# Routed experts in 32-token units with block transposes on VectorE and 21 weight buffers

## The chip, the core and the metric

The kernel runs on one core of a Trainium2 chip. A core has a matrix engine (PE, or TensorE, with a queue for weight loads that the profile lists as PEld), VectorE (DVE), ScalarE (ACT), GpSimd (POOL) and a queue engine SyncE (SP) that only issues DMA transfers here. SBUF holds data in 128 partitions, PSUM takes the matmul results. The metric is the device time of one execution in microseconds (us), the median over runs.

## The reference

One layer of an encoder over 1024 tokens with width 1024: a token mixer, a cross-attention, a mixture of 32 experts, a final norm. Only the experts matter here:

```python
g_logits = (h @ w_rg) + b_rg
p_top, g_idx = lax.top_k(softmax(g_logits), 1)          # 1 of 4 groups
e_top, e_local = lax.top_k(e_logits_of_that_group, 2)   # 2 of its 8 experts
weights = p_top * softmax(e_top)
...
y = (silu(xb @ w_gate[e]) * (xb @ w_up[e])) @ w_down[e]
out = zeros((T, D)).at[t_sorted].add(w_sorted[:, None] * y)
```

All is float32. An expert has w_gate and w_up of 1024 x 512 and w_down of 512 x 1024, 6 MB in all, and 32 of them have to be read from HBM in each execution: 201 MB. 2048 pairs of token and expert are spread over them by the routing, which only the data decide.

## The kernel before, in words

The mixer, the attention and the routing take the first 800 us or so. Behind them comes the expert stage, which is the one that changes.

**Blocks.** The stage walks through 33 blocks in the order of a string, ORDER. A letter says how many tokens of an expert a block can hold: A 96, N 64, B 128. T is an N that takes the first tokens of the busiest expert, and the B behind it the rest of them, with the same weights. The first four blocks (A) work on fixed experts. The later ones look their expert up in a table sorted by load (`perm`), by a register load on SP. Experts that would not fit run in a loop behind the blocks (`For_i`).

**Weights.** The weights of an expert come as 6 loads of 1 MiB, parts 0 to 3 with gate and up columns for two k-tiles of 128 rows each (L926), parts 4 and 5 with the rows of w_down (L928). They go into buffers named `wraw`; SEATS is their number, 20. SP issues the loads in the order of use. `free`, called behind each part, hands the buffer of a finished part to `prep_r`, which issues the next load.

**Tokens.** A gather on POOL (L1081) fetches up to 128 rows of the tokens' states, two blocks ahead. `xpose` turns them by 8 PE transposes (L1165) so that features lie on partitions. Two consecutive N blocks share one gather and one transpose.

**Matmuls.** The tokens are the stationary operand, the weights move. With 64 tokens stationary the array's 128 columns are used as two halves, each with 512 weight columns (`gh`, L1189, and `yh`, L1222). With 32 tokens it is four quarters of 256 weight columns (`gq`, `yq`, the same lines). An A block is a unit of 64 and one of 32 tokens, B two units of 64, N one of 64. `turn` has the units change places from part to part. A matmul of the program is float32 and shows as two records in the trace, each with its weight load.

**Between.** ACT takes silu of the gate columns (L1198), DVE multiplies by the up columns (L1199): `sg`. Then `mpose` brings `sg` into the shape of a stationary operand by PE transposes (L1207) into PSUM, and ACT and DVE copy the result into `mT` (L1210).

**Order on PE.** For block b: parts 0 and 1, the mpose of block b-1, parts 2 and 3, the `xpose` of block b+1, parts 4 and 5 of block b-1 (w_down). The instructions are put in place by a scheduler, but in the main in that order.

**Out.** `store` copies the results from PSUM into a row buffer (L1231; ACT for the unit of 64, DVE for the second unit), multiplies by the routing weight (L1233) and adds the rows to `acc` by an indirect DMA on POOL (L1234). After the last block SP reads `acc` back (L1467), and a last stage normalises and writes the output.

Of the kernel before, what the change touches and what calls it, by code (L numbers as in the profile page):

```python
# [44 lines left out]
ORDER = "AAAA" + "NNN" + "AN" * 4 + "TBN" + "BN" + "AN" * 2 + "AANAANANN"  # L45
NS = ORDER.count("N")
SEATS = 20
# [3 lines left out]
def tile_hybrid_encoder(ctx: ExitStack, tc: tile.TileContext,  # L51
# [1093 lines left out]
    with ExitStack() as pa:  # L1145
        rawp[2] = pa.enter_context(tpool(name="raw5", bufs=SEATS - 11))
        mc = pa.enter_context(tpool(name="mc", bufs=1))
        pgu = pa.enter_context(tpool(name="pgu", bufs=2, space=PSUM))
        xTs = [pp.tile([P, KT, P], F32R, name=n).bitcast(F32) for n in ("xH", "xL")]
        ybuf = [pp.tile([P, KT, P], F32R, name=n).rearrange("p a b -> p (a b)").bitcast(F32) for n in ("xH", "xL")]  # L1150
        xgs += [pp.tile([P, D], F32, name="x1t"), mc.tile([P, D], F32, name="xg")]
        xTn = mc.tile([P, KT, P], F32, name="xTn")
        sgt = mc.tile([P, 512], F32, name="sg")
        mTs = [mc.tile([P, 2, P], F32, name=f"mT{i}") for i in range(2)]
        cnts = {"g": 0, "y": 0, "x": 0}

        def next_gather(tok):
            cnts["g"] += 1
            return gather(xgs[cnts["g"] % 3], tok)
# [9 lines left out]
        def gu_tiles(us):  # L1169
            return [pgu.tile([P, 512], F32, name="gh") if n == 64 else  # L1170
                    pgu.tile([P, 256], F32, name="gq", bufs=1) for n, _, _ in us]

        def y_tiles(us):
            return [py.tile([P, 512], F32, name="yh") if n == 64 else
                    py.tile([P, 256], F32, name="yq", bufs=1) for n, _, _ in us]

        def turn(us, i):

            us = list(enumerate(us))
            return us[::-1] if i % 2 else us  # L1180

        def gu_part(pss, us, xT, r, i):
            r4 = r.rearrange("p (a b c) -> p a b c", a=2, b=2)
            for u, (n, c0, _) in turn(us, i):
                w = 4 * n
                for k in range(2):
                    kt = 2 * i + k
                    for q in range(P // n):
                        nc.tensor.matmul(pss[u][q * n:q * n + n].rearrange("p (b c) -> p b c", b=2),  # L1189
                                         xT[:, kt, c0:c0 + n], r4[:, k, :, q * w:q * w + w],  # L1190
                                         start=kt == 0, stop=kt == KT - 1)

        def silu_mul(pss, us):
            sg = []
# [200 lines left out]
        for i in (1, 2):  # L1395
            nc.gpsimd.memset(xgs[i], 0.0)
# [137 lines left out]
```

## Time and profile before

| What | us |
|---|---|
| median of 3 runs | 1361.46 |
| lowest and highest run | 1360.13, 1365.47 |
| the profiled execution's own time | 1359.35 |
| its span, first to last instruction | 1357.6 |
| first matmul on expert weights | 801.80 |
| end of the expert matmuls | about 1322.6 |
| PE busy in the span | 1263.0 |

The span is the profiler's, and the execution's own time is 1.75 us more. The page gives the busy time per engine, the span in 40 slices with the clock that TensorE was granted and the DMA rate, the queues, and the costliest groups of instructions. Stretches of the span, an engine's waits and its instructions in order of time were read from the trace.

### The profile page before, as it was taken

What the parts mean: (1) busy time and instruction counts of PE and PEld (TensorE: products, weight loads), DVE (VectorE), ACT (ScalarE), POOL (GpSimd) and SP (SyncE); (2) the same over time, 40 slices, a digit from 0 to 9 for tenths busy, and PEclk for the clock granted to TensorE, in tenths of its full rate; (3) what the DMA queues carried; (4) which work ended last, traced back from release to release, by engine and by line L of the source; (5) the groups of instructions that cost most, each with busy time, mean ns of one, the idle gap of its engine ahead of it and who ended that gap; (6) DMA issues with size and microseconds to landing.
All of it is one profiled execution on the core that took longest, in us unless ns stands there. A gap on an engine that the chain in (4) does not pass through costs nothing. (4 is left out here: it accounts for less than half of the span.)

```text
span 1357.6 us, 20099 instructions
## 1 busy us (share of the span) xinstructions
PE 1263.0 (93%) x7616; PEld 839.4 (62%) x7616; DVE 587.4 (43%) x1418; ACT 408.6 (30%) x855; POOL 182.4 (13%) x281
## 2 busy tenths in 40 slices
PE   6999999999898899999999959999999999999980
PEld 6999888888886788888888723333333333333320
DVE  6743465883477765663466631221111111111213
ACT  7722343332474433453222201111111111111112
POOL 2000100000021111110023231111111111110012
PEclk9999999999999999999999969999999999999995
DMA  8810122211698553443783579999999999999966
GB/s 323 287 62 1 37 82 78 98 42 39 217 327 285 204 186 136 164 173 109 277 297 111 192 284 326 396 405 402 401 405 402 410 397 384 393 388 399 393 247 251
DMA packets 85281, 339.63 MB, mean 250 GB/s; under 512 B 11248, under 2 KB 23728, under 8 KB 60608
## 3 DMA queue, kind: packets, MB, share of 16 engines
q1 hardware_dynamic: 72704, 304.53, 58.8%
q0 software_dynamic: 10032, 26.30, 6.7%
q10 hardware_dynamic: 2448, 7.52, 1.4%
q8 instruction: 60, 0.98, 0.3%
q14 instruction: 37, 0.30, 0.1%
HBM read 297.06 MB, written 48.71 MB: 255 GB/s over the span
## 5 line engine op out<-in xcount | busy, mean ns | idle before, releaser
L1222 PE MATMUL yh<-wraw,mT 128*64 128x512 f32 x560 | 133.6, 600 | 1.7 <-ACT mT L1210 1.7
L1189 PE MATMUL gh<-wraw,xTn 128*64 128x512 f32 x512 | 118.8, 596 | 0.0
L111 DVE TENSOR_TENSOR wl<-wraw,wh 128x1024 fp32r<-128x1024 f32 (+2 forms) x72 | 83.1, 1166 | 42.4 <-ACT wh L110 33.5
L102 PE MATMUL mm<-hH,wh 128*128 128x512 f32 x256 | 100.3, 392 | 0.8 <-ACT wh L110 0.8
L103 PE MATMUL mm<-hL,wh 128*128 128x512 f32 x256 | 100.2, 391 | 0.0
L104 PE MATMUL mm<-hH,wl 128*128 128x512 f32 x256 | 100.0, 391 | 0.0
L110 ACT CAST wh<-wraw 128x1024 fp32r<-128x1024 f32 (+2 forms) x72 | 71.4, 1002 | 44.0 <-PE mm L103 29.8
L1189 PE MATMUL gh<-wraw,xL 128*64 128x512 f32 x320 | 82.8, 612 | 0.0
L1222 PEld LDWEIGHTS yh<-wraw,mT 128*64 128x64 f32 x560 | 36.7, 136 | 68.0 <-issue 64.5
L1189 PEld LDWEIGHTS gh<-wraw,xTn 128*64 128x64 f32 x512 | 36.2, 137 | 66.2 <-issue 64.4
L1199 DVE TENSOR_TENSOR sg<-sg,gh 128x256 f32<-128x256 f32 x35 | 14.8, 422 | 127.6 <-ACT sg L1198 127.6
L1189 PE MATMUL gh<-wraw,xH 128*64 128x512 f32 x288 | 67.3, 600 | 0.5 <-DVE xH L1166 0.5
L103 PE MATMUL mm<-wl,hH 128*128 128x384 f32 (+2 forms) x192 | 61.7, 321 | 0.0
L104 PE MATMUL mm<-wh,hL 128*128 128x384 f32 (+2 forms) x192 | 61.6, 321 | 0.0
L102 PE MATMUL mm<-wh,hH 128*128 128x384 f32 (+2 forms) x192 | 61.3, 319 | 0.0
L102 PEld LDWEIGHTS mm<-hH,wh 128*128 128x128 f32 x256 | 48.1, 188 | 10.8 <-ACT wh L110 1.1
L104 PEld LDWEIGHTS mm<-hH,wl 128*128 128x128 f32 x256 | 48.1, 188 | 10.2 <-issue 0.2
L103 PEld LDWEIGHTS mm<-hL,wh 128*128 128x128 f32 x256 | 48.1, 188 | 10.1 <-issue 0.3
L102 PE MATMUL pc<-wh,yh 128*128 128x512 f32 x128 | 50.9, 402 | 3.3 <-ACT yh L110 3.2
L102 PE MATMUL mm<-vH,xH 128*128 128x512 f32 x128 | 53.8, 420 | 0.0
L103 PE MATMUL pc<-wl,yh 128*128 128x512 f32 x128 | 50.9, 399 | 1.6 <-DVE wl L111 1.6
L102 PE MATMUL mm<-aH,xH 128*128 128x512 f32 x128 | 51.1, 399 | 0.0
(410 smaller groups left out, 2522.2 us busy)
## 6 DMA issues: line engine op xcount, KB each, us to landing
wraw<-in_w_gu_dram SPq DMA_DIRECT2D x128, 1024.0 KB
wraw<-in_w_dn_dram SPq DMA_DIRECT2D x64, 1024.0 KB
wraw<-in_w_kv_dram SPq DMA_DIRECT2D x16, 512.0 KB
xt<-in_x_dram SPq DMA_DIRECT2D x16, 512.0 KB
wraw<-in_w_cm_dram SPq DMA_DIRECT2D x16, 512.0 KB
x1t<-x_dram SPq DMA_DIRECT2D x16, 512.0 KB
wraw<-in_w_tm_dram SPq DMA_DIRECT2D x8, 520.0 KB
wraw<-in_w_qT_dram SPq DMA_DIRECT2D x8, 512.0 KB
```

What stands on the lines that cost most here:

```text
L102: nc.tensor.matmul(o, ah, bh, start=first, stop=False)
L103: nc.tensor.matmul(o, ah, bl, start=False, stop=False)
L104: nc.tensor.matmul(o, al, bh, start=False, stop=last)
L110: nc.scalar.copy(h, r)
L111: nc.vector.tensor_tensor(l, r, f32(h), op=ALU.subtract)
L1189: nc.tensor.matmul(pss[u][q * n:q * n + n].rearrange("p (b c) -> p b c", b=2), xT[:, kt, c0:c0 + n], r4[:, k, :, q * w:q * w + w], start=k ...
L1199: nc.vector.tensor_tensor(t, t, pss[u][:, w:2 * w], op=ALU.mult)
L1222: nc.tensor.matmul(pss[u][q * n:q * n + n], lh, r[:, k * 1024 + q * w:k * 1024 + q * w + w], start=i == 0 and k == 0, stop=i == 1 and k == 1)
```

## The change

Every block is made of units of 32 tokens on column quarters: three for A, four for B, two for N. The 32-row units load their tokens as stationary operand for each quarter, and 256 weight columns move. The matmuls of a unit of 64 are thereby replaced by twice as many with half the columns.

Which gate and up columns a quarter takes is new too. Quarter q gets, of each of the four groups t of 128 columns, the 32 columns from 32q on; before it had a contiguous stretch. With that layout, a unit's `sg` (128 partitions, 128 columns) turned in blocks of 32x32 is already the stationary operand for w_down. So `mpose` becomes one `nc.vector.transpose` for the whole block, and the PE transposes and the copies out of PSUM go.

PSUM has three banks for `gu` and three for `y` (a B block takes a further one for its fourth unit), the gathers have two buffers instead of three, and the transposed tokens of an N pair lie in one of the two `xT` tiles. The memory that this sets free goes to a 21st weight buffer. `store` copies four strips per unit, by turns on ACT and DVE. ORDER holds the same letters in another order.

```diff
-ORDER = "AAAA" + "NNN" + "AN" * 4 + "TBN" + "BN" + "AN" * 2 + "AANAANANN"
+ORDER = "AAAA" + "NNA" * 3 + "NTB" + "A" + "NNA" * 2 + "B" + "AANNAAANN"
-SEATS = 20
+SEATS = 21
...
-        return {"A": [(64, 0, 0), (32, 64, 64)], "B": [(64, 0, 0), (64, 64, 64)],
-                "N": [(64, 64 * half_of[b][1] if b in half_of else 0, 0)]}[blocks[b][0] if b is not None else "N"]
+        kind = blocks[b][0] if b is not None else "N"
+        first = 64 * half_of[b][1] if b in half_of else 0
+        return [first + 32 * u for u in range({"A": 3, "B": 4, "N": 2}[kind])]
...
-        pgu = pa.enter_context(tpool(name="pgu", bufs=2, space=PSUM))
+        pgu = pa.enter_context(tpool(name="pgu", bufs=3, space=PSUM))
...
-        xgs += [pp.tile([P, D], F32, name="x1t"), mc.tile([P, D], F32, name="xg")]
-        xTn = mc.tile([P, KT, P], F32, name="xTn")
+        xgs.append(pp.tile([P, D], F32, name="x1t"))
...
-        mTs = [mc.tile([P, 2, P], F32, name=f"mT{i}") for i in range(2)]
+        mT = mc.tile([P, 4, P], F32, name="mT")
...
         def gu_part(pss, us, xT, r, i):
...
+            r6 = r.rearrange("p (a b t q c) -> p a b t q c", a=2, b=2, t=4, q=4)
+            for k in range(2):
+                kt = 2 * i + k
+                for u, c0 in enumerate(us):
+                    for q in range(4):
+                        nc.tensor.matmul(
+                            pss[u][q * 32:q * 32 + 32].rearrange("p (b t c) -> p b t c", b=2, t=4),
+                            xT[:, kt, c0:c0 + 32], r6[:, k, :, :, q], start=kt == 0, stop=kt == KT - 1)
...
         def mpose(sg, us):
-            tp = trt()
-            for u, (n, _, _) in enumerate(us):
-                for j in range(n // 32):
-                    nc.tensor.transpose(tp[:, 2 * u + j], sg[u][:, j * P:(j + 1) * P], ident)
-            for u, (n, _, _) in enumerate(us):
-                m = n // 32
-                (nc.vector.tensor_copy if u else nc.scalar.copy)(mTs[u][:, 0:m], tp[:, 2 * u:2 * u + m])
-            return mTs
+
+            n = len(us) * P
+            nc.vector.transpose(mT.rearrange("p u c -> p (u c)")[:, 0:n], sg[:, 0:n])
+            return mT
...
         def dn_part(pss, us, mm, r, i):
...
+            for k in range(2):
+                ft = 2 * i + k
+                for u in range(len(us)):
+                    for q in range(4):
+                        nc.tensor.matmul(pss[u][q * 32:q * 32 + 32], mm[:, u, ft * 32:ft * 32 + 32],
+                                         r[:, k * 1024 + q * 256:k * 1024 + q * 256 + 256],
+                                         start=ft == 0, stop=ft == 3)
...
+            for u in range(len(us)):
+                for q in range(4):
+                    (nc.vector.tensor_copy if q % 2 else nc.scalar.copy)(
+                        y[u * 32:u * 32 + 32, q * 256:q * 256 + 256], pss[u][q * 32:q * 32 + 32])
...
-        py = pa.enter_context(tpool(name="py", bufs=2, space=PSUM, side="right"))
+        py = pa.enter_context(tpool(name="py", bufs=3, space=PSUM, side="right"))
```

On PE, in one of the first A blocks, the program before has the w_down matmuls of the block before it (`yh`, `yq`) and then its own gate and up matmuls by turns of 64 and 32 tokens, with the PE transposes of `sg` between them:

```order
L1189 MATMUL gh<-wraw,xH 64x512 x4
L1189 MATMUL gq<-wraw,xH 32x256 x16
L1189 MATMUL gh<-wraw,xH 64x512 x4
L1207 MATMUL tp<-ident,sg 128x128 x3
L1189 MATMUL gh<-wraw,xH 64x512 x4
L1189 MATMUL gq<-wraw,xH 32x256 x16
L1189 MATMUL gh<-wraw,xH 64x512 x4
L1165 MATMUL tp<-ident,x1t 128x128 x8
```

In the program after, at the same place and in the first N blocks behind it (`gu` and `y` are now the names of the results for all units):

```order
L1179 MATMUL gu<-wraw,xL 32x256 x96
L1165 MATMUL tp<-ident,x1t 128x128 x8
L1201 MATMUL y<-wraw,mT 32x256 x48
L1179 MATMUL gu<-wraw,xH 32x256 x96
L1165 MATMUL tp<-ident,x1t 128x128 x8
L1201 MATMUL y<-wraw,mT 32x256 x48
L1179 MATMUL gu<-wraw,xL 32x256 x64
L1201 MATMUL y<-wraw,mT 32x256 x48
L1179 MATMUL gu<-wraw,xL 32x256 x64
```

An A block has 96 + 48 matmuls of the program, all 32x256, where it had 16 + 32 for gate and up columns, 8 + 16 for w_down and three transposes of `sg`; no change of shape stands inside it, and nothing of PE stands between the gate and up columns and w_down but the transposes of tokens.

On SP, behind the first lookups of an expert, before (`txt` is the table for T, that SP fetches at its place in the queue; ISA rows are register work):

```order
L928 DMA wraw<-in_w_dn_dram 128x2048 x2
L1349 TENSOR_LOAD perm
L1349 ISA x2
L926 ISA
L926 DMA wraw<-in_w_gu_dram 128x2048
L926 ISA
L926 DMA wraw<-in_w_gu_dram 128x2048
L1298 TENSOR_LOAD perm
L1298 ISA x2
```

And after:

```order
L929 DMA wraw<-in_w_dn_dram 128x2048 x2
L1329 TENSOR_LOAD perm
L1329 ISA x2
L927 ISA
L927 DMA wraw<-in_w_gu_dram 128x2048
L927 ISA
L927 DMA wraw<-in_w_gu_dram 128x2048
L927 ISA
L927 DMA wraw<-in_w_gu_dram 128x2048
L1278 TENSOR_LOAD perm
```

One load more stands ahead of the table; the loads and their order by use are otherwise the same.

## Rows read from the trace of the kernel before

**Rows 1.** The page: busy time of each engine with its share of the span and its number of instructions, and the span in 40 slices with the busy share of PE and the DMA engines' mean busy share in tenths.
```profile
PE 1263.0 (93%) x7616; PEld 839.4 (62%) x7616; DVE 587.4 (43%) x1418; ACT 408.6 (30%) x855; POOL 182.4 (13%) x281
...
PE   6999999999898899999999959999999999999980
DMA  8810122211698553443783579999999999999966
```

**Rows 2.** Stretches of the expert stage: from and to, length; busy us of PE, PEld, DVE, ACT and POOL (instructions); granted clock; DMA share; GB/s.
```profile
797.00:812.00 15.00, 12.10 (x69) 4.72 (x70) 3.68 (x28) 1.87 (x2) 5.44 (x7) 0.70 0.51 153
812.00:835.00 23.00, 22.48 (x190) 9.12 (x193) 4.78 (x20) 2.87 (x7) 2.01 (x2) 1.00 0.90 334
835.00:910.00 75.00, 75.00 (x531) 27.77 (x525) 19.94 (x44) 12.49 (x26) 11.45 (x9) 1.00 1.01 383
910.00:1000.00 90.00, 87.34 (x597) 31.70 (x595) 14.42 (x30) 14.59 (x31) 12.99 (x10) 1.00 1.02 405
1200.00:1296.00 96.00, 94.12 (x694) 33.85 (x692) 18.48 (x40) 14.77 (x32) 9.56 (x7) 1.00 1.01 393
1312.00:1318.00 6.00, 4.30 (x20) 1.26 (x18) 0.42 (x1) 1.09 (x3) 0.00 (x0) 1.00 0.37 116
1318.00:1323.00 5.00, 3.65 (x16) 1.06 (x16) 0.74 (x1) 1.22 (x3) 1.40 (x1) 1.00 0.54 137
```

**Rows 3.** What SP's queue waited for from 803 to 910 us: us in total, times, longest.
```profile
SPq L928 <- PE gq L1189: 24.4, 4, 15.8
SPq L928 <- PE gh L1189: 15.5, 9, 2.3
```

**Rows 4.** The same from 910 to 1300 us.
```profile
SPq L926 <- DMA wraw<-in_w_gu_dram: 107.2, 46, 4.1
SPq L926 <- DMA wraw<-in_w_dn_dram: 80.6, 41, 3.2
SPq L926 <- PE yh L1222: 1.9, 5, 1.0
```

**Rows 5.** What PE waited for from 780 us to the end.
```profile
PE tp L1165 <- DMA x1t<-h,tokt: 8.6, 1, 8.6
PE tp L1207 <- DVE sg L1199: 8.5, 9, 0.9
```

**Rows 6.** SP's instructions in order of time: start, length, line, transfer, how many. Left out between 815.11 and 910.57 are rows with 32 loads, and between 910.57 and 1288.56 rows with 126.
```profile
806.84 3.03 SPq L928 DMA_DIRECT2D wraw<-in_w_dn_dram  x2
815.11 10.26 SPq L926 DMA_DIRECT2D wraw<-in_w_gu_dram  x4
...
910.57 8.13 SPq L926 DMA_DIRECT2D wraw<-in_w_gu_dram  x4
...
1288.56 7.80 SPq L928 DMA_DIRECT2D wraw<-in_w_dn_dram  x4
```

**Rows 7.** PE's instructions in order of time: an A block (837.53 to 855.67) and the rows ahead of it, then an N block (886.76 to 898.76).
```profile
834.78 1.05 PE L1222 MATMUL yq<-wraw,mT 128*32 128x256 f32 x16
835.76 1.94 PE L1222 MATMUL yh<-wraw,mT 128*64 128x512 f32 x8
837.53 1.89 PE L1189 MATMUL gh<-wraw,xL 128*64 128x512 f32 x8
839.34 1.93 PE L1189 MATMUL gq<-wraw,xL 128*32 128x256 f32 x32
841.21 1.94 PE L1189 MATMUL gh<-wraw,xL 128*64 128x512 f32 x8
843.08 0.55 PE L1207 MATMUL tp<-ident,sg 128*128 128x128 f32 x3
...
849.15 1.09 PE L1165 MATMUL tp<-ident,x1t 128*128 128x128 f32 x8
...
855.67 1.89 PE L1189 MATMUL gh<-wraw,xH 128*64 128x512 f32 x8
...
886.76 3.60 PE L1189 MATMUL gh<-wraw,xTn 128*64 128x512 f32 x16
890.30 0.44 PE L1207 MATMUL tp<-ident,sg 128*128 128x128 f32 x2
...
898.76 3.60 PE L1189 MATMUL gh<-wraw,xTn 128*64 128x512 f32 x16
```

**Rows 8.** Groups of instructions by line and shape: number | busy us, mean ns of one.
```profile
L1207 PE MATMUL tp<-ident,sg 128*128 128x128 f32 x85 | 16.7, 295 | 8.5 <-DVE sg L1199 8.5
...
L1231 DVE COPY xH<-yq 32x256 f32<-32x256 f32 x32 | 13.5, 422 | 18.6 <-PE yq L1222 18.2
...
L1166 DVE COPY xL<-tp 128x512 f32<-128x512 f32 x9 | 6.2, 689 | 22.1 <-PE tp L1165 22.1
...
L1199 DVE TENSOR_TENSOR sg<-sg,gq 128x128 f32<-128x128 f32 x15 | 4.3, 288 | 97.0 <-ACT sg L1198 97.0
```

**Rows 9.** The page's queues, the instruction loads of q8: packets, MB, share of 16 engines' span.
```profile
q8 instruction: 60, 0.98, 0.3%
```

**Rows 10.** The end of the stage, all engines in order of time.
```profile
1318.48 0.37 ACT L1210 COPY mT<-tp 128x256 f32<-128x256 f32 x1
...
1318.91 3.65 PE L1222 MATMUL yh<-wraw,mT 128*64 128x512 f32 x16 [1.67 <-ACT mT L1210]
...
1322.61 1.17 ACT L1231 COPY xL<-yh 64x512 f32<-64x512 f32 x2 [3.75 <-PE yh L1222]
```

More of the change, by code (lines that the diff above doesn't have):

```diff
@@ L1158, in next_gather @@
             cnts["g"] += 1
-            return gather(xgs[cnts["g"] % 3], tok)
+            return gather(xgs[cnts["g"] % 2], tok)
         def xpose(xg, xT):
@@ L1167, in xpose @@
             return xT
[L1169 to L1180, printed above, removed]
-        def gu_part(pss, us, xT, r, i):
[L1183 to L1191, printed above, removed]
@@ L1213, in dn_part, with banks @@
-        def dn_part(pss, us, mm, r, i):
-            for u, (n, _, _) in turn(us, i):
-                w = 8 * n
-                for k in range(2):
-                    if n == 64:
-                        lh = mm[u][:, k, i * 64:i * 64 + 64]
-                    else:
-                        lh = mm[u][:, 0, (2 * i + k) * 32:(2 * i + k) * 32 + 32]
-                    for q in range(P // n):
-                        nc.tensor.matmul(pss[u][q * n:q * n + n], lh, r[:, k * 1024 + q * w:k * 1024 + q * w + w],
-                                         start=i == 0 and k == 0, stop=i == 1 and k == 1)
+        def banks(pool, us, name):
+            return [pool.tile([P, 256], F32, name=name) if u < 3 else
+                    trt().rearrange("p a b -> p (a b)")[:, 0:256] for u in range(len(us))]
@@ new lines, in silu_mul @@
+        def silu_mul(pss, us):
+            for u, ps in enumerate(pss):
+                t = sgt[:, u * P:u * P + P]
+                nc.scalar.activation(t, ps[:, 0:P], AF.Silu)
+                nc.vector.tensor_tensor(t, t, ps[:, P:2 * P], op=ALU.mult)
+            return sgt
+        def mpose(sg, us):
+            n = len(us) * P
+            nc.vector.transpose(mT.rearrange("p u c -> p (u c)")[:, 0:n], sg[:, 0:n])
+            return mT
+        def dn_part(pss, us, mm, r, i):
+            for k in range(2):
[5 more added lines that the diff above has]
+                                         start=ft == 0, stop=ft == 3)
@@ L1227, in store @@
             y = ybuf[cnts["y"] % 2]
[L1228 to L1232 removed]
+            for u in range(len(us)):
+                for q in range(4):
+                    (nc.vector.tensor_copy if q % 2 else nc.scalar.copy)(
+                        y[u * 32:u * 32 + 32, q * 256:q * 256 + 256], pss[u][q * 32:q * 32 + 32])
+            n = 32 * len(us)
             nc.vector.tensor_scalar(y[0:n], y[0:n], wt[0:n], None, op0=ALU.mult)
@@ L1412, in tile_hybrid_encoder @@
                 us = parts(b)
-                ps = gu_tiles(us)
+                ps = banks(pgu, us, "gu")
                 for i in range(4):
@@ L1429, in tile_hybrid_encoder @@
                 us = parts(b - 1)
-                ys = y_tiles(us)
+                ys = banks(py, us, "y")
                 for i in range(2):
@@ L1447, in tile_hybrid_encoder @@
             us = parts(None)
-            xd = xpose(next_gather(tx[:, 0:1]), xTn)
-            ps = gu_tiles(us)
+            xd = xpose(next_gather(tx[:, 0:1]), xTs[0])
+            ps = banks(pgu, us, "gu")
             for k in range(4):
@@ L1452, in tile_hybrid_encoder @@
             md = mpose(silu_mul(ps, us), us)
-            ps = y_tiles(us)
+            ps = banks(py, us, "y")
             for k in range(2):
```

22 lines of the change are left out of this document (3 added, 19 removed).

## The prediction

> **What bounds the kernel now.** I read the page's slices first. From about 850 us to the end of the expert stage PE and the DMA engines both stand at 9 tenths [rows 1], so the page alone doesn't say which of them sets the pace. The waits do. From 910 us on SP, which issues the weight loads, waits some 107 and 81 us behind earlier gate/up and w_down loads, and hardly 2 us behind matmuls that hold a buffer [rows 4]. PE in the same stage never waits for a weight load worth a row; its waits are 8.6 us for the first gather and 8.5 us for `sg` [rows 5]. So from 910 us the transfers set the pace of the buffers, and PE is just fast enough not to show it. The loads' cadence says the same: 130 loads between the issue at 910.57 and that at 1288.56 [rows 6], 2.91 us each, with the DMA share at 1.01 to 1.02 and 393 to 405 GB/s [rows 2].
>
> Before 910 us it is otherwise. SP waits there for matmuls of the first blocks, once for 15.8 us [rows 3], since all 20 buffers are full and the first part is not done. The DMA engines move 153, 334 and 383 GB/s in the three stretches from 797 to 910 us, where 405 is shown right behind [rows 2]. Transfer time lost against 405: 15 x (1 - 153/405) = 9.3 us, 23 x (1 - 334/405) = 4.0, 75 x (1 - 383/405) = 4.1; 17.4 us in all. Whatever of this a change recovers shifts the whole later stream of loads, and so the end. What is won on PE after 910 us shifts nothing.
>
> **The change part by part.**
>
> *The 21st buffer.* One load of 1 MiB more is issued before the queue stands still: 1.05 MB at 405 GB/s are 2.6 us. The gap that it fills is there [rows 2, 3]. Gain 2.6 us, at least 0 if the extra load only lengthens the wait behind it.
>
> *32-token units on PE.* The number of units of 32 is 85, one PE transpose of `sg` each before [rows 8]; 15 of them stood alone, so 35 units of 64 existed. A unit of 64 had 48 matmul records (32 for gate and up, 16 for w_down), one of 32 has 96. Before: 35 x 48 + 15 x 96 + 85 = 3205 records, after: 85 x 96 = 8160. The price of one: sixteen 32-token records take 834.78 to 835.76, 0.98 us, and 32 take 839.34 to 841.21, 1.87 us [rows 7]; sixteen more cost 0.89, 55.6 ns each, and the remaining 0.09 belongs to the change of shape. With that share in it, one is 58.4. An A block after: 288 x 55.6 ns + 1.09 for the transposes of tokens = 17.1 us, where the trace shows 837.53 to 855.67 = 18.14. It loses three PE transposes of 0.55 and the changes of shape, and gains 1.0 us; at 58.4 ns the gain is 0.2. An N block: 192 x 55.6 = 10.7, with the transposes 11.8, against 12.0 [rows 7].
>
> The first four blocks are A and lie in the stretch where PE holds the buffers, so 4 x 1.0 = 4 us of their gain pass to the loads (1 us at 58.4 ns; the stretch has 17.4 - 2.6 = 14.8 left to give). I take 4. In the rest PE is merely earlier and then waits: its whole work is 8160 x 55.6 ns = 454, plus some 25 token transposes x 1.09 = 27, plus 4.5 that the first 15 us lose at the granted clock of 0.70 [rows 2]: 486 us, in a stage that lasts from 801.8 to 1322.6, 520.8 us. 35 us of PE become idle, in waits of a microsecond or so ahead of a part. I cost them at nothing, since stretches with PE busy 4.30 of 6 and 3.65 of 5 us still had a granted clock of 1.00 [rows 2].
>
> *Block transposes on DVE.* The trace has none. The nearest rows are a multiply of 128x128 in 288 ns and a copy of 128x512 out of PSUM in 689 ns [rows 8], so 0.3 to 1.4 us for an A block, allowing twice the copy. It lies behind the multiplies of block b, and w_down of b comes only after the gate and up part of b+1, over 7 us later; DVE is busy 18.5 of 96 us [rows 2]. On the path it stands only in the last block, where it replaces a PE transpose (0.44) and a copy (0.37): nothing. The 8.5 us that PE waited for `sg` [rows 5] go, into the same idle time.
>
> *Copies of the results.* 85 x 4 copies of 32x256 at 422 ns [rows 8] are 143 us, half on ACT and half on DVE, beside 510 us of matmuls. Three banks each for `gu` and `y`: gate and up of b+1 need the banks of b, and between lie the w_down records of b-1, 64 or 96 x 55.6 = 3.6 to 5.3 us. Silu and multiply of three units take about 2 us, and PE has spare time for the rest. Nothing; without the spare time, up to 0.5 us x 33 = 16 us.
>
> *Strided columns.* The runs that move are 32 columns long instead of 128. No row shows runs as short. Zero if a column costs a cycle wherever it lies; otherwise it goes into the rate below.
>
> *The end.* The last loads are issued by 1296.4 [rows 6], and the DMA rate has fallen to 116 GB/s from 1312 us [rows 2], so the last w_down part is about there when PE starts. Before it, PE waits 1.67 us for the copy of `mT`, which stood behind copies of the results on ACT [rows 10]. The copy goes; 0 to 1.67 gained, and I take 1.2, the larger half, since 64 short records and shorter copies follow it. The output behind stays.
>
> *SP.* The order of the loads is the same, one load further ahead. *Code.* 4955 more matmul records, each with a weight load, are 9910 instructions; 0.98 MB for 2 x 7616 of them are 64 bytes each [rows 1, 9], so 0.63 MB or 39 more packets of q8. The 60 of before took 0.3% of 16 x 1357.6 us, 1.09 us of one DMA engine each. Spread evenly, 39 x 1.09 / 16 = 2.7 us; if all fell on an engine that the loads wait for, 42 us; nothing, if on one that waits for others. I take nothing, as the cadence of 2.91 us already holds such packets, and keep 42 as the far end. The Trainium skill, "Runtime: NRT & Kernel Launch", section "Instruction fetch mechanics", calls the crossing of a 16 KiB block mostly hidden; by it this term is nothing too, though it speaks of the engine that fetches, not of the transfers beside it. No row here shows the latter.
>
> Sum: 2.6 + 4 + 1.2 = 7.8 us off the profiled execution's 1359.35: 1351.6. The median of the runs is 2.1 above that execution, so 1353.7 against 1361.46. Its own range: from all 17.4 + 1.67 gained (1342) to the gain of a buffer alone less the 2.7 of the code (1361).
>
> **The rivals.**
>
> *PE's instruction rate (the slower side).* The sum of 55.6 ns rests on a run of 32 records with 32 weight loads. An A block on average shows 155 records (48, 96, 3 and 8) in 18.14 us, 117 ns each [rows 7], so no row shows PE taking two instructions each 55.6 ns for long. If the rate that lasts is r, the stage is 8160 r + 32 us; it decides from (520.8 - 32) / 8160 = 59.9 ns on. At 64 ns: 554 us, 33 more, 1395; at 70 it is 82 more. For it: 8160 records where 3205 were, and runs of 96 to 192 without pause. Against it: nothing in the bursts slows down. The Trainium skill, "TensorE: Matmul & The Clock Gate", section "Wait — 56ns, not 53.3ns?", gives a matmul about 62 ns in the sequencer when its hardware decode is off, and a floor of about 25 ns otherwise; by the first the stage would be 538 us and the median 1379, by the second nothing changes, and the 55.6 ns of the burst speak for the second.
>
> *Instruction loads hold up the weights.* 39 packets, each 1.09 us of one engine, half of them in front of a load that the others wait for: 21 us, net 13 slower: 1375. For it: the DMA engines are full [rows 2] and each load is split over all of them. Against: a share of 0.3% [rows 9].
>
> *No gain.* The extra buffer only moves the wait and the token transposes or banks eat what PE gains in the first blocks, while the loads behind 910 us keep their 2.91 us: within 4 us of before, 1358 to 1363. For it: all gain hangs on one stretch of 110 us.
>
> **How the numbers follow.** Forecast 0.45, instruction loads 0.20, rate 0.19, no gain 0.16. A measurement of this kernel can tell about 0.5%, 6.8 us, from no change, so faster is below 1354.7 and slower above 1368.3. Of the forecast 0.31 lies below and 0.14 above that bound; of the instruction loads 0.04 below, 0.04 between, 0.12 above; of the rate 0.02, 0.02 and 0.15; of no gain 0.04, 0.09 and 0.03. Together faster 0.41, same 0.29, slower 0.30. The range from 1345 to 1386 leaves out a rate above some 63 ns and a gain above 16 us.
>
> **What would show it.** Right: SP's row of 15.8 us behind the first matmuls shorter, 405 GB/s reached earlier than 910 us, the cadence still 2.9 us, an A block of the start in 17 us, and PE with new waits for `wraw`. The rate shows itself as gate and up runs of 60 ns and more per record with no wait in them, and loads that again wait for PE after 910 us. Instruction loads would show as a cadence of 3.0 us or more with PE waiting for weights. The prediction is wrong if PE gets slower in the first blocks, or if the cadence changes at all.

## The result and the profile after

The changed kernel takes 1369.86 us (median of 6 runs, 1367.84 to 1374.03) where the kernel before takes 1361.46. The ratio is 1.0058 with a 95% interval of 1.0043 to 1.0073: slower by 8.4 us, where 7.8 us less was forecast. The profiled execution takes 1370.82 us, its span is 1369.1.

Where the 11.5 us between the two profiles lie follows from five marks in the traces: the start of the last attention matmul (`mm<-vH`), the start of the first expert matmul, the issue of load 58 and of load 191 (the last, counted from 0) on SP, the end of the last expert matmul, and the end of the span. In us:

| Stretch | before | after |
|---|---|---|
| up to the last attention matmul | 774.6 | 780.5 |
| to the first expert matmul | 27.2 | 30.1 |
| to the issue of load 58 | 108.8 | 101.9 |
| to the issue of load 191 | 385.5 | 394.5 |
| to the end of the expert matmuls | 26.5 | 25.2 |
| to the end | 35.1 | 36.9 |
| last five together | 583.1 | 588.5 |

The first row is chance. In its stretch the engines' instructions stand in the same order in both kernels, and it came out between 773.2 and 781.6 us in the fourteen profiles of this study (776.5 in a second one of the kernel before). The other rows are the change: 2.9 us lost ahead of the first matmul, 6.9 won behind it, 9.0 lost while the transfers are saturated, 1.3 won and 1.8 lost at the end. They come to 5.4 us, where the medians differ by 8.4. Each profile is one execution (the second one of the kernel before has 582.2 us in the last five rows), and some 3 us of the 8.4 stand in no row.

The page of the changed kernel, busy time by engine, the DMA slices and the code loads, answers to [rows 1, 9]:

```profile
span 1369.1 us, 30309 instructions
...
PE 1245.6 (91%) x12571; PEld 948.0 (69%) x12571; DVE 649.6 (47%) x1575; ACT 425.5 (31%) x961; POOL 179.7 (13%) x280
...
DMA  8820022311698653453773389999999999999966
...
q8 instruction: 100, 1.64, 0.5%
```

PE is busy for 17 us less, with 4955 more matmuls, and the code loads of q8 rise from 60 packets to 100. The stretches answer to [rows 2], with 780 to 790 us added:

```profile
780.00:790.00 10.00, 4.42 (x31) 3.44 (x30) 6.69 (x33) 1.30 (x3) 0.98 (x3) 0.83 0.26 107
...
797.00:812.00 15.00, 3.23 (x24) 2.21 (x28) 1.94 (x9) 1.21 (x2) 5.14 (x6) 0.50 1.01 418
812.00:835.00 23.00, 22.59 (x362) 12.90 (x358) 5.82 (x37) 2.08 (x5) 3.06 (x4) 0.96 0.84 319
835.00:910.00 75.00, 74.80 (x1329) 44.77 (x1325) 27.80 (x64) 16.12 (x45) 11.43 (x9) 1.00 1.01 394
910.00:1000.00 90.00, 83.82 (x1438) 50.03 (x1432) 27.32 (x62) 17.84 (x51) 14.81 (x12) 0.96 1.02 400
...
1200.00:1296.00 96.00, 87.67 (x1474) 50.09 (x1464) 28.94 (x65) 18.66 (x53) 10.47 (x8) 0.98 1.01 385
```

The DMA engines stand nearly idle from 780 to 790 us (0.26) and are full from 797 to 812, the reverse of before, where the same two stretches show 1.01 and 0.51 [rows 2]:

```profile
780.00:790.00 10.00, 1.94 (x10) 1.61 (x9) 7.79 (x50) 0.48 (x3) 1.08 (x1) 0.50 1.01 404
```

From 835 to 910 us they move 394 GB/s in place of 383, as hoped. From 910 us on it is 400 for 405 and then 385 for 393.

What SP did at the start, in the kernel before (rows that stand ahead of [rows 6]: start, length, line, transfer, how many):

```profile
769.32 5.76 SPq L926 DMA_DIRECT2D wraw<-in_w_gu_dram  x3
775.13 0.90 SPq L928 DMA_DIRECT2D wraw<-in_w_dn_dram  x2
776.07 14.88 SPq L926 DMA_DIRECT2D wraw<-in_w_gu_dram  x4
```

And in the changed kernel, with the last two rows of its stage:

```profile
775.29 14.88 SPq L927 DMA_DIRECT2D wraw<-in_w_gu_dram  x3
790.22 1.15 SPq L929 DMA_DIRECT2D wraw<-in_w_dn_dram  x2
791.41 1.99 SPq L927 DMA_DIRECT2D wraw<-in_w_gu_dram  x4
794.33 21.10 SPq L929 DMA_DIRECT2D wraw<-in_w_dn_dram  x2
...
1287.85 8.70 SPq L927 DMA_DIRECT2D wraw<-in_w_gu_dram  x4
1302.73 4.66 SPq L929 DMA_DIRECT2D wraw<-in_w_dn_dram  x4
```

Loads 12 to 19 used to be issued from 770 to 791 us; now load 12 holds SP until 790 and the rest come in a burst behind it. At the end SP stands still for 6 us ahead of the last four loads. The waits of SP's queue name both causes, from 740 to 800 us and from 910 to 1305 us; the row between them, from 803 to 910 us, answers to [rows 3]:

```profile
SPq L927 <- DMA h<-hn: 13.5, 1, 13.5
...
SPq L929 <- PE gu L1179: 34.6, 11, 18.3
...
SPq L927 <- DMA wraw<-in_w_gu_dram: 110.4, 47, 4.4
...
SPq L929 <- DMA gfb<-in_g_final_dram: 6.0, 1, 6.0
```

The first wait is for a tile called `hn`, the normed states of the last 128 tokens, that has to be stored to `h` before its memory may be overwritten. The last is for `gfb`, the gains of the final norm, a load of 512 KB. The longest wait for matmuls of the first blocks has grown from 15.8 to 18.3 us, where the prediction looked for a shorter one. Which buffer lies on `hn` is read from the addresses in the built programs (bytes within a partition):

```
work5 (attention): pr 130080 and 134176, hn 138272 and 142368
raw5 before: 9 buffers of 8192 from 64544, the last at 130080
raw5 after: 10 buffers from 64544, the last at 138272
addresses in the order of the first loads:
  before: load 11 64544, load 12 130080, 13 121888, ... 19 72736
  after:  load 11 64544, load 12 138272, 13 130080, ... 20 72736
```

The pool hands out its second buffer from the top. So the 21st buffer is not the last to be filled but the second of its pool, and it lies on the last tile of the attention that becomes free.

PE's own waits from 780 us to the end answer to [rows 5]:

```profile
PE tp L1165 <- DMA x1t<-h,tokt: 11.8, 1, 11.8
PE tp L1165 <- DMA x1t<-h,tkr: 11.3, 3, 6.2
PE gu L1179 <- DMA wraw<-in_w_gu_dram: 9.4, 10, 2.1
PE y L1201 <- DMA wraw<-in_w_dn_dram: 7.3, 6, 2.8
```

The first gather is waited for 3.2 us longer; later gathers and, for the first time, the weights are waited for as well. The second A block and its neighbours answer to [rows 7]:

```profile
842.95 10.54 PE L1179 MATMUL gu<-wraw,xL 128*32 128x256 f32 x192
853.43 1.09 PE L1165 MATMUL tp<-ident,x1t 128*128 128x128 f32 x8
854.45 5.39 PE L1201 MATMUL y<-wraw,mT 128*32 128x256 f32 x96
859.65 10.54 PE L1179 MATMUL gu<-wraw,xH 128*32 128x256 f32 x192
```

A block takes 842.95 to 859.65, 16.7 us where it took 18.14. A record costs (853.43 - 842.95) / 192 = 54.6 ns in a run of 192.

### The profile page after: what moved, and what is told of

Read it like the earlier page. It is cut to its first block, busy times and chain, and to the rows that moved or that the text cites. A ratio compares the mean times of both kernels' runs of the same rounds, so it can differ in the third digit from the quotient of the medians.

```text
span 1369.1 us, 30309 instructions
## 1 busy us (share of the span) xinstructions
PE 1245.6 (91%) x12571; PEld 948.0 (69%) x12571; DVE 649.6 (47%) x1575; ACT 425.5 (31%) x961; POOL 179.7 (13%) x280
## 5 line engine op out<-in xcount | busy, mean ns | idle before, releaser
L1179 PE MATMUL gu<-wraw,xL 128*32 128x256 f32 x2880 | 167.4, 384 | 5.9 <-DMA wraw<-in_w_gu_dram 5.2
L1201 PE MATMUL y<-wraw,mT 128*32 128x256 f32 x2656 | 157.8, 385 | 11.3 <-DMA wraw<-in_w_dn_dram 7.3
L1179 PE MATMUL gu<-wraw,xH 128*32 128x256 f32 x2432 | 142.4, 380 | 4.1 <-DMA wraw<-in_w_gu_dram 4.1
L1179 PEld LDWEIGHTS gu<-wraw,xL 128*32 128x32 f32 x2880 | 95.2, 111 | 70.7 <-DMA wraw<-in_w_gu_dram 7.8
L1201 PEld LDWEIGHTS y<-wraw,mT 128*32 128x32 f32 x2656 | 86.5, 111 | 71.3 <-issue 15.1
L1179 PEld LDWEIGHTS gu<-wraw,xH 128*32 128x32 f32 x2432 | 81.4, 110 | 55.7 <-DMA wraw<-in_w_gu_dram 4.9
L1187 DVE TENSOR_TENSOR sg<-sg,gu 128x128 f32<-128x128 f32 x83 | 23.7, 288 | 175.9 <-ACT sg L1186 169.1
L1210 DVE COPY xL<-y 32x256 f32<-32x256 f32 x86 | 36.3, 422 | 86.8 <-ACT xL L1210 84.7
L1210 DVE COPY xH<-y 32x256 f32<-32x256 f32 x80 | 33.8, 422 | 73.7 <-ACT xH L1210 71.7
L1210 ACT COPY xL<-y 32x256 f32<-32x256 f32 x86 | 31.2, 363 | 83.3 <-PE y L1201 58.5
```

The costliest lines, as they stand in the source:

```text
L1179: nc.tensor.matmul(pss[u][q * 32:q * 32 + 32].rearrange("p (b t c) -> p b t c", b=2, t=4), xT[:, kt, c0:c0 + 32], r6[:, k, :, :, q], start ...
L1187: nc.vector.tensor_tensor(t, t, ps[:, P:2 * P], op=ALU.mult)
L1201: nc.tensor.matmul(pss[u][q * 32:q * 32 + 32], mm[:, u, ft * 32:ft * 32 + 32], r[:, k * 1024 + q * 256:k * 1024 + q * 256 + 256], start=ft ...
L1210: (nc.vector.tensor_copy if q % 2 else nc.scalar.copy)(y[u * 32:u * 32 + 32, q * 256:q * 256 + 256], pss[u][q * 32:q * 32 + 32])
```

## The experiments

Each is told with its ratio to the kernel before. The medians of the kernel before beside them were 1362.2 to 1362.4.

**The start and the end: a, b, c, d.** Run a gives the buffer on `hn` a pool of its own, so that it is the last of the first 21; run b moves the load of `gfb`; run c does both; run d goes back to 20 buffers.

```diff
-    seats = [0] * 6 + [1] * 5 + [2] * (SEATS - 11)
+    seats = [0] * 6 + [1] * 5 + [2] * (SEATS - 12) + [3]
...
-        rawp[2] = pa.enter_context(tpool(name="raw5", bufs=SEATS - 11))
+        rawp[2] = pa.enter_context(tpool(name="raw5", bufs=SEATS - 12))
+        rawp[3] = pa.enter_context(tpool(name="raw6", bufs=1))
```

> The changed kernel with its 21st weight buffer in a pool of its own, so that it is the last of the first 21 loads that takes the memory of the late tile hn and not the second of the ten in that pool. Theory start (eight first loads stand behind one that waits for hn): the loads of the start are issued from about 775 to 791 us again, the DMA share from 780 to 790 us goes from 0.26 to over 0.9, the first gather is waited for some 3 us less, and the median falls by 3 to 6 us, to 1364 to 1367. Theory cadence alone (9 us lost in 2.98 us per load in place of 2.91): the start changes, but the median stays within 2 us of 1369.9, as the loads run at the same rate behind it.

```diff
-        nc.scalar.dma_start(gfb, rowb(g_final, 0, D))
+        nc.gpsimd.dma_start(gfb, rowb(g_final, 0, D))
```

> The changed kernel with the load of the final norm's gains (gfb) issued from POOL instead of ACT, so that it takes none of the places that the weight loads wait on. Theory end (the last four weight loads wait 6 us behind gfb): SP's wait for gfb goes, the last four loads are issued 3 to 6 us earlier, and the median falls by 1 to 4 us. Rival: the DMA engines were full at 1.03 and 0.99 in that stretch, so the last load lands when it did; within 1 us of 1369.9.

> Both of these edits in the changed kernel. If start and end are separate losses, their gains add up: 1360 to 1366, and what stays above 1361.5 is the cadence. If the cadence alone matters: 1368 or more.

```diff
-SEATS = 21
+SEATS = 20
```

> The changed kernel with 20 weight buffers, so that the memory of the start is laid out as in the kernel before; the units, transposes and the order of the blocks are the new ones. Theory start: the first loads are issued as in the kernel before, median 1363 to 1367. Theory cadence (instruction loads): the loads from the 58th to the 184th still stand 2.96 to 3.0 us apart. Rival to it, that the 21st buffer or the start makes the cadence: 2.91.

Measured: a 1368.84 (1.0052, 1.0035 to 1.0068), b 1368.25 (1.0044, 1.0026 to 1.0061), c 1365.74 (1.0020, 1.0008 to 1.0032), d 1363.45 (1.0014, 1.0002 to 1.0026). In a the loads of the start are issued as before and the DMA share from 780 to 790 us is 0.99, but the gather is still waited for 11.0 us, so the median stays within the bounds of the rival. In b the median is 1.6 us lower, in its theory's range of 1 to 4, and SP's wait for `gfb` is gone; the first of the last four loads is issued 5.3 us earlier after the last attention matmul, but the last of them only 0.4 us (526.1 for 526.5). Neither edit alone stands clear of the changed kernel's interval; both together do, 4.1 us less, within the 1360 to 1366 of two separate losses. The profiles, one execution each, do not repeat this: the last five rows come to 588.5 us in the changed kernel and 588.0 in c. Taking the 21st buffer away takes 6.4 us off: in d the first gather is waited for 7.1 us, `gfb` happens to be placed behind the last loads, and the last five rows come to 584.7 us. In c `gfb` is still issued ahead of the last weights, at 1284.8 us; its 512 KB are 1.3 us at 405 GB/s, an estimate. The new units, transposes and ORDER alone thus cost 1 to 2 us, not 8. The loads from 58 to 191 take 394.4 (a), 393.8 (b) and 394.1 us (c), and 390.3 in d. From load 58 to 184, of which d's expectation speaks, it is 369.4 us, 2.93 for each load: between the 2.96 of the one theory and the 2.91 of the other.

**The cadence: e, f, g.** Run e cuts the matmuls of 64-token units in the kernel before, f takes ORDER back, g the grouped columns, both with 20 buffers.

```diff
-                        nc.tensor.matmul(pss[u][q * n:q * n + n].rearrange("p (b c) -> p b c", b=2),
-                                         xT[:, kt, c0:c0 + n], r4[:, k, :, q * w:q * w + w],
-                                         start=kt == 0, stop=kt == KT - 1)
+                        o4 = pss[u][q * n:q * n + n].rearrange("p (b c) -> p b c", b=2)
+                        for j in range(4 if n == 64 else 1):
+                            m = slice(j * 64, j * 64 + 64) if n == 64 else slice(0, w)
+                            nc.tensor.matmul(o4[:, :, m], xT[:, kt, c0:c0 + n],
+                                             r4[:, k, :, q * w + m.start:q * w + m.stop],
+                                             start=kt == 0 and j == 0, stop=kt == KT - 1 and m.stop == w)
...
+                        for j in range(0, w, m):
+                            nc.tensor.matmul(pss[u][q * n:q * n + n, j:j + m], lh,
```

> The kernel before with each matmul of a 64-token unit cut into four of 128 weight columns: 8245 expert matmul records in place of 3205, nearly the 8160 of the changed kernel; the units, the columns that move in all, the transposes, the order of the blocks and the 20 buffers are the old ones. Theory instruction loads: the loads from the 58th to the 191st take 390 us as in the changed kernel with 20 buffers, where the kernel before has 385.5, and the median rises by 3 to 6 us, to 1365 to 1368. Rival, that the weights are read twice as often by 32-token units, or their order: 385 to 386, and a median within 2 us of 1362.3.

```diff
-ORDER = "AAAA" + "NNA" * 3 + "NTB" + "A" + "NNA" * 2 + "B" + "AANNAAANN"
-SEATS = 21
+ORDER = "AAAA" + "NNN" + "AN" * 4 + "TBN" + "BN" + "AN" * 2 + "AANAANANN"
+SEATS = 20
```

> The changed kernel with 20 buffers and ORDER of the kernel before. Theory order of the blocks (the new order makes the loads of the later part slower or PE wait for gathers): loads 58 to 191 take 386 us in place of 390.3, PE's waits for gathers (11.5 us) go, and the median falls by 2 to 4 us from 1363.5. Rival, instruction loads or reads: 390 and 1363 to 1365.

```diff
-SEATS = 21
+SEATS = 20
...
-            r6 = r.rearrange("p (a b t q c) -> p a b t q c", a=2, b=2, t=4, q=4)
+            r5 = r.rearrange("p (a b q c) -> p a b q c", a=2, b=2, q=4)
...
-                            xT[:, kt, c0:c0 + 32], r6[:, k, :, :, q], start=kt == 0, stop=kt == KT - 1)
+                            xT[:, kt, c0:c0 + 32], r5[:, k, :, q], start=kt == 0, stop=kt == KT - 1)
```

> The changed kernel with 20 buffers, the gate and up columns of a quarter contiguous as before (runs of 128 columns) in place of groups of 32. The products with w_down are then formed with the features in another order, so the experts' result is another one; all instructions and their sizes stay. Theory strided reads cost: the stretch from load 58 to 191 shortens by 2 us or more and the median falls to 1361 or less. Rival: no change, 1362.5 to 1364.5.

In f the two N blocks of a pair no longer stand side by side, and the second then works on the tokens of the block ahead of it; the same holds for run h below. The work of the engines is the same in amount.

Measured: f 1365.91 (1.0027, 1.0011 to 1.0044), g 1365.48 (1.0029, 1.0013 to 1.0045). The loads from 58 to 191 take 392.3 and 391.2 us. Neither median is clear of d, and both lie above the ranges that were expected, the rivals' too. The order of the blocks and the grouped columns thus explain none of the loss; PE waits for later gathers under the old ORDER too (7.3 and 4.6 us).

Run e went another way: 1460.63 (1.0720). Both theories of it are missed, since PE became the bound: in the run below, 32 records of 128 columns with 64 tokens take 2.5 us, 78 ns each (75 on average over the stage, 505.4 us of PE for 6720),

```profile
1029.81 2.57 PE L1192 MATMUL gh<-wraw,xTn 128*64 128x128 f32 x32
1032.31 0.66 PE L1165 MATMUL tp<-ident,x1t 128*128 128x128 f32 x4
```

where a quarter of an old record costs (890.30 - 886.76) / 64 = 55 [rows 7]. As a test of the median it is void. One stretch of it still serves in part, 910 to 1000 us, in which the DMA engines were full. The row of the stretch in e:

```profile
910.00:1000.00 90.00, 90.00 (x1276) 80.68 (x1273) 14.82 (x31) 13.19 (x28) 12.74 (x10) 1.00 1.02 400
```

It shows 400 GB/s at a share of 1.02, as the changed kernel does, with the old units' reading of the weights, the old transposes, the old ORDER and 20 buffers. What e shares with the changed kernel is a much larger number of PE instructions (1276 matmul records in the stretch and 1438 in the changed kernel, 597 before). The code loads in that stretch, first in e:

```profile
DMA packets 5653, 36.03 MB, mean 400 GB/s; under 512 B 916, under 2 KB 916, under 8 KB 1615
...
q8 instruction: 10, 0.16, 0.7%
```

and in the kernel before:

```profile
DMA packets 5772, 36.47 MB, mean 405 GB/s; under 512 B 918, under 2 KB 918, under 8 KB 1734
...
q8 instruction: 5, 0.08, 0.3%
```

In all fourteen profiles the same stretch has 404 to 406 GB/s with 5 code packets (the kernel before twice, h and i below) and 400 or 401 with 10 to 12 (e and the nine kernels with the new units). So in this stretch the rate goes with the code loads, by 1.1%, and the code's own bytes take another 0.3% from the weights. Over 910 to 1275 us it is 398 GB/s with 18 packets before, 396 in d and 395 in the changed kernel with 46; from 1100 to 1200 us alone the two kinds overlap (389 to 395 with the old units, 386 to 395 with the new). That the code loads cause it is not shown by e: SP waited there for buffers, some 70 us, the weights themselves moved no slower (32.98 MB on SP's queue for 33.02 before), and rows take a different share of the engines in each kernel (12.4% in e, 13.7% before, 15.6% in the changed kernel).

The packets of the traces say more. From 910 to 1275 us a weight packet of 8192 bytes that was in flight within half a us of a code load, and of no row transfer, took 322.9 ns before and 321.7 in d; one away from both took 316.0 and 316.4. So the weights are slower beside a code load and as fast as before elsewhere, which speaks against a cause that works all the time, such as what PE reads. Beside a code load stand 1100 packets before and 2922 in d.

**The buffer and the first gather: h, i, j, k, l.** Run h gives the kernel before 21 buffers (with the pool of run a), by the same means as the change: two gather buffers, no `xTn`. Runs i, j and k hold the last of the first loads on SP until the first gather has landed.

```diff
-        xgs += [pp.tile([P, D], F32, name="x1t"), mc.tile([P, D], F32, name="xg")]
-        xTn = mc.tile([P, KT, P], F32, name="xTn")
+        xgs.append(pp.tile([P, D], F32, name="x1t"))
...
-SEATS = 20
+SEATS = 21
```

> The kernel before with the freed memory alone: two gather buffers, the tokens of an N pair in one of the two tiles, 21 weight buffers of which the 21st is used last at the start. Units, PE transposes and order of the blocks stay. Theory of the prediction (each MB more of buffers starts the stream 2.6 us earlier): 1358 to 1361. Rival, that a 21st buffer only delays the first gather and gives nothing: 1362 to 1365.

```diff
-        prep_r(SEATS)
+        prep_r(SEATS - 4)
         route_p(NT - 1, c)
         route_t(NT - 1, c)
         xg[0] = gather(xgs[0], tokt[:, 0:1])
+        nc.sync.dma_start(hold_dram, xgs[0][0:1, 0:1])
+        prep_r(SEATS)
```

> The kernel before with its last four first loads (16 to 19) held on SP until the first gather has landed, by a transfer of 4 bytes that reads the gathered tile. Theory start (the table scatters and the first gather of the experts wait in the DMA engines behind weight loads, and PE's stretch of 521 us from the first to the last expert matmul begins when that gather lands): PE's wait for the first gather falls from 8.6 us to 2 to 5, the first expert matmul comes 4 to 7 us earlier after the last attention matmul (27.2 us before), and the median is 1356 to 1359. Rival, that the loads held back are missed later: 1362 or more, with PE waiting for wraw.

> The changed kernel with 20 buffers and the same four loads held. If the transfers set the end there and the DMA engines stand idle for 10 us less at the start: 1358 to 1361, 3 to 5 less than the 1363.5 without the hold. If the loads are what is late: 1363 or more.

> The changed kernel with 21 buffers (the 21st used last, gains loaded from POOL) and five loads held until the first gather has landed. If the 21st buffer's only harm was one more load in front of the first gather, this is at least as fast as the same with 20 buffers: 1357 to 1361. If a further buffer gives nothing: 1361 to 1364.

> The kernel before once more, for a second profile of it. If the 6 us by which the changed kernel's profile is late at the last attention matmul (780.5 against 774.6) are chance, this one has that matmul between 776 and 781; if the changed kernel is really later there, at 774 to 776. The stretches behind it should repeat within 2 us: 27 us to the first expert matmul, 521 from there to the last, 35 to the end.

Measured: h 1364.17 (1.0012, 0.9994 to 1.0029), i 1357.99 (0.9966, 0.9953 to 0.9979), j 1362.56 (1.0010, 0.9997 to 1.0024), k 1365.89 (1.0024, 1.0008 to 1.0041), l 1360.43 in one run.

Run h: the 21st buffer wins nothing in the kernel before. Its load stands in front of the first gather, which is waited for 11.3 us in place of 8.6, and the first expert matmul comes 29.9 us after the last attention matmul in place of 27.2. At the end `gfb` holds SP in h as well:

```profile
SPq L928 <- DMA gfb<-in_g_final_dram: 11.1, 1, 11.1
```

PE has no wait for weights in h even so, so this wait cost it nothing there.

Run i is faster than both kernels, as its first theory had it. What it changes is seen on POOL. The kernel before, with the two scatters of the routing table and the first gather (L1081):

```profile
787.11 1.08 POOL L1076 DMA_INDIRECT tab_dram<-val,dst  x1 [7.81 <-issue]
792.98 0.98 POOL L1076 DMA_INDIRECT tab_dram<-val,dst  x1 [4.79 <-DMA tab_dram<-val,dst]
794.27 1.07 POOL L1081 DMA_INDIRECT x1t<-h,tokt  x1 [0.30 <-issue]
```

And run i:

```profile
792.08 1.08 POOL L1077 DMA_INDIRECT tab_dram<-val,dst  x1 [7.50 <-issue]
794.57 0.98 POOL L1077 DMA_INDIRECT tab_dram<-val,dst  x1 [1.41 <-DMA tab_dram<-val,dst]
795.86 1.06 POOL L1082 DMA_INDIRECT x1t<-h,tokt  x1 [0.30 <-issue]
```

The scatter lands sooner (1.41 us of wait in place of 4.79), the gather too; what the edit took away is the weight loads in front of them. PE's wait for it in run i:

```profile
PE tp L1166 <- DMA x1t<-h,tokt: 4.0, 1, 4.0
```

It is 4.0 us for 8.6, the first expert matmul comes at 22.3 us, and the end 4.4 us earlier. The held loads are not missed: PE has no wait for `wraw`. From there on run i takes as long as the kernel before:

| From the last attention matmul, us | before | l | h | i | after | c | d | j | k |
|---|---|---|---|---|---|---|---|---|---|
| to the first expert matmul | 27.2 | 27.3 | 29.9 | 22.3 | 30.1 | 29.5 | 27.1 | 22.5 | 22.3 |
| from there to the end of the last | 520.8 | 519.9 | 520.9 | 520.2 | 521.5 | 522.0 | 520.8 | 527.8 | 525.8 |
| from there to the end | 35.1 | 35.0 | 35.1 | 35.2 | 36.9 | 36.5 | 36.8 | 36.8 | 36.9 |

With the old units (before, l, h, i) the expert matmuls take 520 to 521 us whenever they start. With the new ones (j, k) an earlier start of 4 to 8 us is lost again by the end. Both expectations of j and k are missed: j is 0.9 us below d and k no better than c. What they lose is seen by counting the 8192-byte packets of the weight loads, 128 for each, that have landed at a given time after the last attention matmul, against the kernel before. In loads ahead (+) or behind:

| Time after | l | h | i | after | d | j | k |
|---|---|---|---|---|---|---|---|
| 20 us | -0.1 | 0.0 | -2.8 | -3.1 | -0.1 | -2.8 | -2.8 |
| 135 us | +0.4 | +0.3 | +1.9 | +1.4 | +1.5 | +1.5 | +2.2 |
| 300 us | +0.4 | -0.2 | +1.9 | +0.2 | +0.6 | +0.4 | +1.1 |
| 500 us | +0.3 | -1.0 | +1.6 | -0.5 | +0.1 | -0.3 | +0.6 |
| 520 us | +0.4 | -1.4 | +1.5 | -1.3 | +0.2 | -0.1 | 0.0 |

The changed kernel does get its lead, 1.4 loads or 4.1 us at 2.9 us each, in spite of the bad start, and then loses all of it and more. Run i keeps 1.5 of its 1.9. All nine kernels with the new units lose 1.4 to 2.7 loads between 135 and 520 us, l and i 0 to 0.4. Run h, with the old units, loses 1.7; SP waits there for buffers that PE still holds, once for 4.4 us, and near the end for `gfb`.

## Why the prediction was wrong

**What bounds.** Half of the reading failed. I took the transfers as what sets the end from 910 us on and wrote that what is won on PE after 910 us shifts nothing. That SP waits for its own earlier loads [rows 4] says that the engines are full, not that PE waits for them, and PE did not [rows 5]. The kernel before was bound by both within a few us, and it was PE that ended last. It was busy for 505 of the 518 us of the stage:

```profile
806.00:1324.00 518.00, 505.13 (x3405) 184.07 (x3397) 98.32 (x228) 81.42 (x173) 70.61 (x55) 1.00 0.98 381
```

The last weight packet landed at 1318.3 us, 2.4 us before the first matmul that reads that load. Runs h and i move the start of the expert matmuls by +2.7 and -4.9 us, and the end follows with 520.9 and 520.2 us between. A wait for the first gather stood in [rows 5] with 8.6 us, the largest row of PE, and I gave it no term. In the changed kernel the reading holds: PE waits for `wraw`, and an earlier start of PE gains nothing that stands clear (j against d, k against c).

**The 21st buffer, 2.6 us forecast as a gain.** This step failed most, and its lower bound of 0 too: by the medians the buffer costs 6.4 us (1369.86 with it, 1363.45 in d). "One load of 1 MiB more is issued before the queue stands still" counts buffers and doesn't ask where the further one lies or what is in front of the gather. Even where it is used last it gains nothing (h, c): the queue then stands still longer for the first part, 18.1 us in h and 17.1 in c for 15.8 [rows 3], and that part comes later, since the load is one more in front of the first gather. This gather was waited for 11.0 to 11.8 us in the five kernels with 21 buffers and no hold, 7.0 to 9.9 in those with 20. In the changed kernel the buffer lies on `hn`, its load is the second of the pool's, and SP waits 13.5 us for it; that place adds 0.8 us to the gather's 11.0 of a. How the 6.4 us divide over the place, `gfb` and the load itself is not shown: by the medians a takes 1.0 off, c 3.1 more and d 2.3 more, of which only the 3.1 is clear of noise. Without the buffer the change costs 1.2 us by the medians of d and of the kernel before beside it (0.3 to 3.5 by the interval), and not 8.4.

**The first A blocks, 4 us.** Right. An A block takes 16.7 us for 17.1 worked out, and from the last attention matmul to load 58 it is 132.5 us in d, at 20 buffers, for 136.0 before: 3.5 us. In all, load 58 came 4.0 us earlier in the changed kernel (132.0). This gain did not reach the end.

**The cadence, forecast unchanged at 2.91 us.** Failed. By the issues it is 2.97 in the changed kernel (394.5 / 133) and 2.93 in d, against 2.90 (385.5 / 133). Issues also hold single waits, so that h, with the old units, has 394.3 us too. A straight line through the landings of the 45th to the 175th MiB of the weights gives 2.88 or 2.89 us for each with the old units (before, l, h, i) and 2.91 to 2.93 in all nine kernels with the new ones, with 20 buffers or 21. This is the rival of the instruction loads in place and sign: more code packets, PE waiting for weights. It was sized at 21 us; the lead lost is 1.4 loads in d, some 4 us. The term that I took as nothing lies near its evenly spread end of 2.7 us. Some 2.5 us can be followed in d: from 910 to 1275 us the code's share of the engines is 0.8% for 0.3%, 1.8 us, and 1822 more weight packets stand beside a code load, each some 6 ns longer, 0.7 us over 16 engines. The rest is open. The engine that fetches the code does not wait for it: PE's runs of 192 records go through at 54.6 ns. The Trainium skill, "Runtime: NRT & Kernel Launch", section "Instruction fetch mechanics", calls the cost of crossing a 16 KiB block of code mostly hidden; for PE that agrees with these 54.6 ns, and the cost seen here lies with the transfers that share the DMA engines, of which the section doesn't speak.

**The end, 1.2 us.** Failed in sign. The copy of `mT` does go. In its place the load of `gfb` came to stand among the last weight loads, with 6.0 us of wait (gone in b), and the tail is 1.8 us longer. The last two blocks show why: PE waits for the two engines that empty its banks, and each unit's four strips are copied behind the other unit's:

```profile
1328.15 0.64 PE L1201 MATMUL y<-wraw,mT 128*32 128x256 f32 x8 [0.94 <-ACT xH L1210]
...
1329.01 3.23 PE L1201 MATMUL y<-wraw,mT 128*32 128x256 f32 x56 [0.22 <-DVE xH L1210]
...
1331.92 1.66 ACT L1210 COPY xL<-y 32x256 f32<-32x256 f32 x4 [3.02 <-PE y L1201]
1332.31 1.78 DVE L1210 COPY xL<-y 32x256 f32<-32x256 f32 x4 [2.12 <-ACT xL L1210]
1334.12 0.74 DVE L1213 TENSOR_SCALAR xL<-xL,wtr 64x1024 f32<-64x1024 f32 x1
```

I had costed copies and banks at nothing because PE had time to spare; in the last block nobody has. From 1331.92 to 1334.1 the copies take 2.2 us, where two of ACT took 1.17 [rows 10]. What sets the tail is the scatter of the block before the last, whose rows are copied as slowly. Before and after:

```profile
1319.51 1.40 POOL L1234 DMA_INDIRECT acc<-xH,tkr  x1 [10.40 <-DVE xH L1233]
1324.84 1.40 POOL L1234 DMA_INDIRECT acc<-xL,tkr  x1 [3.93 <-DVEq L1438]
...
1330.94 1.41 POOL L1214 DMA_INDIRECT acc<-xH,tkr  x1 [15.24 <-DVE xH L1213]
1336.36 1.41 POOL L1214 DMA_INDIRECT acc<-xL,tkr  x1 [4.01 <-DMA acc<-xH,tkr]
```

The last scatter starts 5.3 and 5.4 us behind it, in the changed kernel by a wait for it to land. It went out 3.1 us ahead of the end of the last matmul before and 1.3 us ahead of it after; the difference is the 1.8 us. In d the tail is all of the loss: from the last attention matmul to the end of the expert matmuls it takes 547.9 us there and 548.0 before.

**Transposes, columns, the rate.** Right. The block transposes on DVE take 569 and 424 ns, within the bounds of 0.3 to 1.4 us:

```profile
L1193 DVE STREAM_TRANSPOSE mT<-sg 128x384 f32<-128x384 f32 x15 | 8.5, 569 | 0.3
...
L1193 DVE STREAM_TRANSPOSE mT<-sg 128x256 f32<-128x256 f32 x16 | 6.8, 424 | 0.0
```

No wait for them appears. The grouped columns cost nothing that g could show. The rival of PE's rate is out: 54.6 ns in runs of 192, below the 59.9 from which it decides. The Trainium skill, "TensorE: Matmul & The Clock Gate", section "Wait — 56ns, not 53.3ns?", has 62 ns per matmul for the case without hardware decode; these runs speak against that case here. The clock was not untouched by the waits, where I had said 1.00: it is 0.96 from 910 to 1000 us. The level of 1.2 GHz (0.51) stands from 981 to 988 us, and PE waited for a gather from 978.2 to 984.4; from 1131 to 1135 (0.57) it stands behind waits for weights, from 1234 to 1237 (0.50) behind another gather. At that level 32 records take 3.19 us in place of 1.93. What this costs the end is not shown.

What stays open: how much of the slower stream is due to the code loads and how much to whatever else the new units do; how the 6.4 us of the buffer divide; what PE's waits for later gathers (11.3 us) cost, since no run gave the changed kernel its third gather buffer back; and why k, with the best lead of the new units at 300 us and the gather early, still ends 3.3 us behind j by the medians (their intervals overlap).

## What to carry to other kernels

A further prefetch buffer is worth what its first load waits for: look up where it lies, which tile leaves that memory last, and what stands behind its load in an in-order queue. A small transfer on the critical path, a gather here, should be issued ahead of the megabytes that can wait; holding four loads for it gave 4.4 us without touching any matmul, in the kernel in which PE ended last, and nothing clear in the one that waits for its weights. And where transfers set the pace, ask what more instructions cost them: here a stream of weights more than 1% slower went with 2.5 times the instructions of PE in the stage, although no engine waited for its code.

## What was not expected of the hardware

Matmuls of 64 tokens with 128 columns cost 75 to 78 ns each (run e), with the queue of weight loads busy for 80.7 of 90 us; within matmuls of 512 columns the same array work cost 55 ns, and 32-token matmuls of 256 columns also 54.6. Cutting the moving side to a quarter was dear with 64 tokens stationary, while halving both sides was free.

A scatter of the routing table had to be waited for 4.79 us with weight loads issued ahead of it and 1.41 us without them: the loads ahead held a small transfer up by 3.4 us.

A weight packet beside a code load took some 6 ns longer than one away from it (322.9 against 316.0 ns before, 321.7 against 316.4 in d).
